# Ranks for the mixers' small matmuls, products grouped by tile size, and activation tiles moved to one byte remainder

## The chip, the cores and the metric

The kernel runs on one core of one Trainium2 chip. The metric is device time in microseconds (us) of one launch; the runs shown are medians of repeated launches. Engines are named as the profile names them: PE (TensorE matmul), PEld (TensorE weight load), DVE (VectorE), ACT (ScalarE), POOL (GpSimd), SP (the queue that issues most DMAs).

## The reference

One sequence of 256 positions and width 1024 passes through two model blocks, all in float32.

- The first block has two layers. A layer is a SwiGLU feed-forward (inner width 2816) added with weight 0.5, then a mixer, then a second such feed-forward. The mixer projects the normalized input to three groups of heads, runs them side by side (16 heads of a Mamba-2 state-space form in chunks of 128, called ssd; 4 mLSTM heads of 128; 8 RWKV-7 heads of 64) and projects their outputs back.
- The second block is one layer: a modulation from a vector `c`, eight attention heads of 64 beside a gated convolution, an output projection, and a feed-forward with a 3-tap convolution.

The part of ssd that the change rewrites is, per chunk of 128 positions and per head,

```
y_diag = einsum(cb * decay, x_dt)        # within a chunk
y_off  = einsum(C, state_before) * exp(a_cum)   # from the state before the chunk
y      = y_diag + y_off + X * d_skip
```

## The kernel before, in words

Activations are kept transposed: 128 features on the partitions, 256 positions along the row. A weight matrix is cut into 128x128 blocks, 3,808 in all, streamed in chunks of seven (`raw`, 448 KB) by SP. `chunk` (L126) splits a chunk into a rounded high part `whi` (ACT, L134) and the rest `wlo` (DVE, L135). `mm` (L151) then issues three matmuls for one block, all of 128x128 weights against 256 columns: high by high (L153), high by low (L154), low by high (L155). The activations they multiply lie in tiles that hold a high and a low part: `pair0` and `pair1` (a normalized input), `hp` (the hidden layer of a feed-forward, 22 blocks of 256 columns, one tile in each of the five feed-forwards), and ring tiles `w` in a mixer. They are called weight matmuls below, 11,424 in all. Every other matmul is small, in plain float32, and part of some chain of dependent steps.

The mixer (`mixers`, L385) weaves five chains into the projections: `rwkv` twice (L518, four heads each), `gates` (L795), `ssd` (L980), `mlstm` (L849). Each chain is a generator that yields an estimated cost; `weave` (L487) resumes the chain whose estimated time is least if that is not later than the projections' own estimated time, else it writes the next projection. So the program text alternates. The order in which instructions stand on an engine is then set by the Tile framework's scheduler: among instructions that its own model of the program holds ready, the one with the lowest rank goes first, and the rank is the position in the written order. `tc.high_priority(n)` lowers the rank by n. Before, a chain's step is moved up by `BOOST`, one position (L500). Each engine then runs its instructions strictly in that order.

The steps named below: in `rwkv`, L691 multiplies the pieces of a 64x64 triangular inverse (its input comes from a solve in 15 steps on DVE and a reordering on ACT), L704 and L705 finish a level; L633 and L642 are small sums and transposes; then a recurrence over four chunks runs L726/L729 (products into `x1`), a copy `R` on ACT (L732), L736, a copy on ACT (L737), L742 and L754, and the new state on DVE (L747, L750). In `ssd`, for each of four groups of four heads, L1064 and L1066 are the products within the first and the second chunk and L1068 the product with the state.

A matmul uses only part of the array if it has fewer than 128 rows to sum over or fewer than 128 outputs. The profile prints this part as rows*columns: weight matmuls 128*128, L1064 and L1066 128*64 (64 outputs), L1068, L691, L704, L705, L729 and L736 64*64, L601 64*128. This is called the tile size below.

`gap` (L258) allocates an unused tile of n bytes per partition in a pool and clears it on POOL. It shifts the start of all tiles that are allocated behind it. As built, `whi` and `wlo` start 160 bytes past a multiple of 256; the starts of the activation tiles are listed with the change. The calls that the change resizes are at L324, L397, L1164, L1271, L1314 and L1316.

Of the kernel before, what the change touches and what calls it, by code (L numbers as in the profile page):

```python
# [16 lines left out]
T = 256  # L17
# [20 lines left out]
GD_AHEAD = 1  # L38
BOOST = (1, 1, 1, 1, 1)
DENSE = 0.34  # L40
GAPS = {"xg": 448, "xn": 192, "mix": 288, "ffn": (384, 128, 448, 192, 448), "attn": 256}
W_OUT = ((("rwkv0", "rwkv1"), (12, 13, 14, 15)), (("ssd",), (0, 1, 2, 3, 4, 5, 6, 7)), (("mlstm",), (8, 9, 10, 11)))

IN_PAIRS = "k0 r0 v0 r2 k2 v2 xb8 xb0 dtg xb2 xb4 xb6 z0 z2 z4 xm0 z6 xm2 o0 o2".split()
# [33 lines left out]
def _program(tc, a, order, dbg=None):  # L78
    nc = tc.nc
    es = ExitStack()  # L80
    dbg = dbg or (lambda name, ap: None)
    V, S, G, PE = nc.vector, nc.scalar, nc.gpsimd, nc.tensor

    def pool(name, bufs=1, **kw):
        return es.enter_context(tc.tile_pool(name=name, bufs=bufs, **kw))
# [19 lines left out]
    p = ps.tile([128, 512], F32, name="st")  # L105
# [3 lines left out]
    def P(name, j=0, n=1):  # L109
        c = PCOL[name] + j  # L110
        return par[:, c:c + n]
# [96 lines left out]
    def mps(shape=(128, 512), tag="m"):  # L208
        return ps.tile(list(shape), F32, name=tag, bufs=4 if tag == "m" else 1)
# [48 lines left out]
    def gap(pool, n):  # L258
        if n:
            turn.append(0)  # L260
            G.memset(pool.tile([128, n // 4], F32, name=f"gap{len(turn)}"), 0.0)
# [3 lines left out]
    def pair(dtype=F32R):  # L265
        pairs.append(0)
        return act.tile([128, 2, DT, T], dtype, name=f"pair{len(pairs) % 2}")
# [4 lines left out]
    def new_acc():  # L272
        return act.tile([128, 2, T], F32, name="acc", bufs=2)
# [21 lines left out]
    def cut(t, js):  # L295
        return t[:, js[0]:js[-1] + 1]
# [24 lines left out]
    def ffn(l, which, acc, xg, next_gain):  # L321
        with tc.tile_pool(name=f"ffn{which}{l}", bufs=1) as fp:
            gu, dn = f"ffn{which}_w_gate_up", f"ffn{which}_w_down"
            gap(fp, GAPS["ffn"][2 * l + which - 1])  # L324
            hp = fp.tile([128, 2, FT, T], F32R, name="hp")
# [56 lines left out]
    def bc(ap, shape):  # L382
        return ap.to_broadcast(shape)

    def mixers(l, acc, xg):  # L385
# [10 lines left out]

        gap(mp, GAPS["mix"])  # L397
        nka = mp.tile([128, 4], F32, name="nka")
# [79 lines left out]
        for i, (need, ks) in enumerate(W_OUT):  # L478
            last = i == len(W_OUT) - 1
            for js in OUTS if last else ((0, 1), (2, 3), (4, 5), (6, 7)):  # L480
                work.append((None, need, DENSE * len(ks) * len(js), lambda js=js, ks=ks, last=last: w_out(js, ks, last)))
        weave(work, [rwkv(l, 0, mp, ring, b), rwkv(l, 1, mp, ring, b), gates(l, mp, ring, b),
                     ssd(l, mp, ring, b), mlstm(l, mp, ring, weight, b)])
        mx.close()
        return nxt

    def weave(work, gens):  # L487
        done, now = {}, 0.0
        chains = [[0.0, g, None, i] for i, g in enumerate(gens)]
        work = list(work)  # L490
        while work or chains:
            free = [c for c in chains if c[2] is None or c[2] in done]
            c = min(free, key=lambda c: max(c[0], done.get(c[2], 0.0))) if free else None
            if c:
                c[0] = max(c[0], done.get(c[2], 0.0))
            ready = work and all(n in done for n in work[0][1])
            if c and (not ready or c[0] <= now):
                c[2] = None
                try:
                    with tc.high_priority(BOOST[c[3]]):  # L500
                        r = next(c[1])
                except StopIteration as e:
                    chains.remove(c)
                    done[e.value] = c[0]
                    continue
                if isinstance(r, str):
                    c[2] = r
                else:
                    c[0] += r * CHAIN
            else:  # L510
                name, need, cost, fn = work.pop(0)
                now = max([now] + [done[n] for n in need])
                fn()
                now += cost
                if name:
                    done[name] = now
# [463 lines left out]
    def ssd(l, mp, ring, b):  # L980
# [4 lines left out]
        for c in range(2):  # L985
            for g in range(2):
                gs = slice(g * 64, g * 64 + 64)
# [6 lines left out]
        p = mps()  # L994
# [8 lines left out]
        ea = [ring(128, 4, 128) for _ in range(2)]  # L1003
# [7 lines left out]
        xdt = {}  # L1011
        pst = mps()
        for g in range(2):
            yield f"xb{4 * g + 2}"
            hs = slice(g * 8, g * 8 + 8)
            for c in range(2):
                p = mps()
# [11 lines left out]
        st = ring(128, 8, 64)  # L1029
# [8 lines left out]
        def load(q):  # L1038
            if q < 4:
                gds[q] = [ring(128, 4, 128) for _ in range(2)]  # L1040
                for c, t in enumerate(gds[q]):
                    nc.sync.dma_start(t, da[q * 4:q * 4 + 4, c * 128:c * 128 + 128].unsqueeze(0)
                                      .to_broadcast([128, 4, 128]))
# [3 lines left out]
        for q in range(4):  # L1047
            g = q // 2
            gs = slice(g * 64, g * 64 + 64)
            load(q + GD_AHEAD)  # L1050
            gd = gds[q]
            for c, t in enumerate(gd):
                for h in range(4):
                    S.activation(t[:, h], t[:, h], AF.Relu, scale=-1.0, bias=nat[:, c, q * 4 + h:q * 4 + h + 1])
                S.activation(t, t, AF.Exp, scale=-1.0)
                V.tensor_mul(t, t, bc(cbm[:, c, g:g + 1], [128, 4, 128]))
                yield 2.0
            js = (2 * q, 2 * q + 1)
            p = mps()
            for u, i in enumerate(js):  # L1060
                for j in range(2):
                    h = 2 * i + j
                    o = p[j * 64:j * 64 + 64, u * T:u * T + T]
                    PE.matmul(o[:, 0:128], xdt[0, g][:, h % 8], gd[0][:, h % 4], start=(u == 0), stop=True,  # L1064
                              skip_group_check=True)
                    PE.matmul(o[:, 128:256], xdt[1, g][:, h % 8], gd[1][:, h % 4], start=False, stop=False,  # L1066
                              skip_group_check=True)
                    PE.matmul(o[:, 128:256], st[gs, h % 8], ea[h % 8 // 4][gs, h % 4], start=False, stop=True,  # L1068
                              skip_group_check=True)
            for u, i in enumerate(js):  # L1070
                V.scalar_tensor_tensor(xs[:, i], xs[:, i], P(f"ssd_d{l}", i), p[:, u * T:u * T + T],
                                       op0=OP.mult, op1=OP.add)
            yield f"z{2 * q}"
            V.tensor_mul(cut(xs, js), cut(xs, js), cut(b["sz"], js))
            if q % 2 == 0:
                S.activation(accs[g], cut(xs, js), AF.Square)
            else:
                sq = ring(128, 2, T)
                S.activation(sq, cut(xs, js), AF.Square)
                V.tensor_add(accs[g], accs[g], sq)  # L1080
            yield 2.0
# [57 lines left out]
    def modulate(rb, gain, shift):  # L1139
        xn = pair()  # L1140
        for j in range(DT):
            n = tmp()[:, 0]
            V.scalar_tensor_tensor(n, x[:, j], gain[:, j:j + 1], rb, op0=OP.mult, op1=OP.mult)
            S.activation(xn[:, 0, j], n, AF.Identity, bias=shift[:, j:j + 1])
            V.scalar_tensor_tensor(xn[:, 1, j], n, shift[:, j:j + 1], xn[:, 0, j].bitcast(F32),
                                   op0=OP.add, op1=OP.subtract)
        return xn
# [12 lines left out]
    def second(accs, xg):  # L1160
        rb, rb2 = stat_rstd(accs, D, EPS, chain=True)
        with tc.tile_pool(name="attn", bufs=1) as mp:
            xn = modulate(rb2, a1[:, 0], mod[:, 0:8])
            gap(mp, GAPS["attn"])  # L1164
            mixed = [mp.tile([128, 2, 4, T], F32R, name=f"m{i}") for i in range(2)]
# [102 lines left out]
        with tc.tile_pool(name="ffn_2", bufs=1) as fp:  # L1268
            rb, = stat_rstd([acc], D, EPS)
            xn = modulate(rb, a1[:, 1], mod[:, 24:32])  # L1270
            gap(fp, GAPS["ffn"][4])  # L1271
            hp = fp.tile([128, 2, FT, T], F32R, name="hp")
# [40 lines left out]
    acc = new_acc()  # L1313
    gap(act, GAPS["xg"])  # L1314
    xg = pair()
    gap(act, GAPS["xn"])  # L1316
    for j in range(0, DT, 2):
# [8 lines left out]
    later = None  # L1326
    for l in range(LAYERS):
        acc, xg = ffn(l, 1, acc, xg, f"mix_norm{l}")
        dbg(f"xa{l}", x)
        acc, xg = mixers(l, acc, xg)  # L1330
        dbg(f"xb{l}", x)
        if l == LAYERS - 1:
            later = pool("later")
            ab = later.tile([128, 8, 384], F32, name="ab")
        acc, xg = ffn(l, 2, acc, xg, f"ffn1_norm{l + 1}" if l + 1 < LAYERS else None)
        dbg(f"xc{l}", x)
# [161 lines left out]
```

## Time and profile before

| | us |
|---|---|
| median of 3 runs | 1627.86 (1627.2 to 1629.0) |
| the profiled execution, its own time | 1627.1 |
| its span from first to last instruction | 1625.3 |
| PE busy | 1584.9 (98%), 13,660 records |
| PEld busy | 1516.4 (93%) |
| DVE busy | 1161.4 (71%) |
| ACT busy | 1000.1 (62%) |
| POOL busy | 47.5 (3%) |

The profiled execution's own time is 1.8 us above its span, and 0.8 us below the median of the runs. Matmuls overlap in the array, so a busy PE is no PE at its peak: the distance from one matmul's start to the next one's tells more than its duration. A small float32 matmul leaves two records, a transpose one. The program goes through: feed-forward of layer 0 to 196 us, mixer to 474, feed-forward to 658, feed-forward of layer 1 to 845, mixer to 1119, feed-forward to 1306, attention to 1437, last feed-forward to the end.

### The profile page before, as it was taken

Reading aid. Unit: us, or ns where it says so; the run is one execution under the profiler, and the core shown is the slowest. Engines: PE = TensorE matmul, PEld = TensorE weight load, DVE = VectorE, ACT = ScalarE, POOL = GpSimd, SP = SyncE. Lnnn points to the kernel's source line nnn. Section 1 sums busy time; section 2 is a strip of 40 time slices with the busy share of each in tenths; the row PEclk is TensorE's granted clock in tenths of the full one; section 3 lists DMA queues with packets and bytes.
Section 4 is the critical chain, followed back from the end, with each engine's and each line's share of the span. In section 5 each row is a group of like instructions: output and inputs, shape, how many; then the busy total and the mean of one; then the engine's idle time right before and its main releaser. Section 6 shows DMA issues by size and latency. Waiting matters only on the chain.

```text
span 1625.3 us, 33775 instructions
## 1 busy us (share of the span) xinstructions
PE 1584.9 (98%) x13660; PEld 1516.4 (93%) x13660; DVE 1161.4 (71%) x1965; ACT 1000.1 (62%) x1692; POOL 47.5 (3%) x68
## 2 busy tenths in 40 slices
PE   8999999999999999999999899999999999999998
PEld 7999988878999999999998887799999998999997
DVE  7865679856787755787568975688785676798853
ACT  6554576887655454545458788765554566587753
POOL 0000001000000000000000100000000000000000
PEclk9999989999999999999999999999999999999999
DMA  7866633333357766597563333436886653556662
GB/s 252 306 195 190 204 118 123 101 112 116 115 181 244 242 187 194 185 329 260 183 194 125 115 106 117 127 117 216 288 306 185 185 166 113 159 162 190 187 189 72
DMA packets 106717, 290.81 MB, mean 179 GB/s; under 512 B 15640, under 2 KB 28096, under 8 KB 106432
## 3 DMA queue, kind: packets, MB, share of 16 engines
q1 hardware_dynamic: 106272, 288.12, 55.9%
q8 instruction: 107, 1.75, 0.4%
q10 hardware_dynamic: 288, 0.52, 0.1%
q14 instruction: 50, 0.41, 0.1%
HBM read 287.51 MB, written 1.09 MB: 178 GB/s over the span
## 4 chain that ended last, share of the span: by engine, by line
PE 77%; issue 13%; DVE 5%; ACT 2%; DMA 1%; POOL 1%; SPq 0%; DVEq 0%; POOLq 0%; ACTq 0%
PE d L155 21%; PE d L153 21%; PE d L154 21%; DVE wlo L135 1%; DMA ada<-ada 1%; PE m L691 1%; PE m L754 1%; PE m L1064 1%; POOL stm L212 1%; PE m L1068 1%; PE m L736 1%; PE st L221 1%; PE m L705 1%; ACT whi L134 1%; PE m L1066 1%
## 5 line engine op out<-in xcount | busy, mean ns | idle before, releaser
L135 DVE TENSOR_TENSOR wlo<-raw,whi 128x896 fp32r<-128x896 f32 x544 | 590.4, 1089 | 245.1 <-ACT whi L134 242.3
L153 PE MATMUL d<-pair,whi 128*128 128x256 f32 x2672 | 753.2, 282 | 4.8 <-ACT whi L134 2.1
L155 PE MATMUL d<-pair,wlo 128*128 128x256 f32 x2672 | 753.8, 282 | 1.8 <-DVE wlo L135 1.8
L154 PE MATMUL d<-pair,whi 128*128 128x256 f32 x2672 | 752.9, 282 | 0.1
L134 ACT CAST whi<-raw 128x896 fp32r<-128x896 f32 x544 | 511.5, 943 | 348.3 <-PE d L154 254.0
L153 PEld LDWEIGHTS d<-pair,whi 128*128 128x128 f32 x2672 | 508.8, 190 | 14.8 <-issue 5.9
L155 PEld LDWEIGHTS d<-pair,wlo 128*128 128x128 f32 x2672 | 508.1, 190 | 7.2 <-DVE wlo L135 2.9
L154 PEld LDWEIGHTS d<-pair,whi 128*128 128x128 f32 x2672 | 508.5, 190 | 3.0 <-issue 1.4
L154 PE MATMUL d<-hp,whi 128*128 128x256 f32 x880 | 246.6, 280 | 0.0
L155 PE MATMUL d<-hp,wlo 128*128 128x256 f32 x880 | 246.1, 280 | 0.0
L153 PE MATMUL d<-hp,whi 128*128 128x256 f32 x880 | 246.1, 280 | 0.0
L155 PEld LDWEIGHTS d<-hp,wlo 128*128 128x128 f32 x880 | 166.2, 189 | 0.0
L154 PEld LDWEIGHTS d<-hp,whi 128*128 128x128 f32 x880 | 166.1, 189 | 0.0
L153 PEld LDWEIGHTS d<-hp,whi 128*128 128x128 f32 x880 | 166.1, 189 | 0.0
L205 ACT CAST hp<-h 128x256 fp32r<-128x256 f32 x88 | 35.4, 406 | 90.9 <-DVE h L345 90.8
L1124 DVE SCALAR_TENSOR_TENSOR adasum<-ada,sc,adasum 128x1024 f32<-128x1024 f32 x42 | 53.8, 1281 | 14.4 <-DMA ada<-ada 14.4
L206 DVE TENSOR_TENSOR hp<-h,hp 128x256 fp32r<-128x256 f32 x88 | 36.7, 421 | 15.3 <-ACT hp L205 14.5
L1157 DVE SCALAR_TENSOR_TENSOR up<-raw,par,up 128x255 f32<-128x255 f32 (+1 forms) x88 | 37.2, 480 | 10.6 <-ACT raw L1153 10.3
L344 ACT ACTIVATE s<-d 128x256 f32<-128x256 f32 x80 | 30.2, 378 | 23.3 <-PE d L155 22.2
L345 DVE TENSOR_TENSOR h<-s,d 128x256 f32<-128x256 f32 x88 | 36.0, 415 | 3.8 <-ACT s L344 3.8
L155 PE MATMUL d<-w,wlo 128*128 128x256 f32 x128 | 37.1, 290 | 0.0
L154 PE MATMUL d<-w,whi 128*128 128x256 f32 x128 | 37.1, 290 | 0.0
(403 smaller groups left out, 1829.0 us busy)
## 6 DMA issues: line engine op xcount, KB each, us to landing
raw<-ws SPq DMA_DIRECT2D x544, 448.0 KB, 3.7
ada<-ada SPq DMA_DIRECT2D x48, 512.0 KB, 5.9
w<-da SPq DMA_DIRECT2D x16, 256.0 KB, 5.1
w<-small SPq DMA_DIRECT2D x10, 256.0 KB, 3.9
ab<-abias SPq DMA_DIRECT2D x1, 1536.0 KB, 7.1
x<-xT SPq DMA_DIRECT2D x4, 256.0 KB, 4.9
w<-da SPq DMA_DIRECT2D x8, 128.0 KB, 3.6
w<-dw SPq DMA_DIRECT2D x4, 256.0 KB, 5.5
```

Of the source, the lines that this page charges most:

```text
L134: S.copy(hi, raw)
L135: V.tensor_sub(lo, raw, hi.bitcast(F32))
L153: PE.matmul(p, h, xh, start=start, stop=False, skip_group_check=True)
L154: PE.matmul(p, h, xl, start=False, stop=False, skip_group_check=True)
L155: PE.matmul(p, lo, xh, start=False, stop=stop, skip_group_check=True)
L205: S.copy(hi, src)
L206: V.tensor_sub(lo, src, hi.bitcast(F32))
L212: G.tensor_tensor(dst, m, mhalf.to_broadcast([128, n]), op=OP.pow)
L344: S.activation(s, p[:, 0], AF.Silu)
L345: V.tensor_mul(h, s, p[:, 1])
L1124: V.scalar_tensor_tensor(acc, w, sc[:, k:k + 1], acc, op0=OP.mult, op1=OP.add)
L1157: V.scalar_tensor_tensor(dst[:, i, d:], raw[:, i, :T - d], P(w, 3 * j + k), dst[:, i, d:], op0=OP.mult, op1=OP.add)
```

## The change

Three edits.

1. Ranks. `PE` becomes an object whose `matmul` and `transpose` pass through `first`. While `weave` resumes a chain, `PE.chain` is set, and each small matmul of the chain gets a rank far ahead of all others (100,000 less its running number, so that the written order is kept among them). So a chain's matmul that the scheduler's model holds ready goes ahead of every weight matmul, and ahead of matmuls of other chains that were written later.
2. The ssd products. For each group of four heads, all eight products within the chunks are issued first, and the four products with the state behind them. It was one head after the other.
3. Gaps. Sizes change, one is added (`later`), two become nothing.

```diff
-GAPS = {"xg": 448, "xn": 192, "mix": 288, "ffn": (384, 128, 448, 192, 448), "attn": 256}
+AHEAD_PE = 100000
+GAPS = {"xg": 192, "xn": 192, "mix": 32, "ffn": (128, 128, 128, 0, 0), "attn": 0, "later": 256}
...
-    V, S, G, PE = nc.vector, nc.scalar, nc.gpsimd, nc.tensor
+    V, S, G = nc.vector, nc.scalar, nc.gpsimd
+
+    class Ordered:
+
+        chain = False
+        n = 0
+
+        def first(self, op, *args, **kw):
+            if not self.chain:
+                return op(*args, **kw)
+            self.n += 1
+            with tc.high_priority(AHEAD_PE - self.n):
+                return op(*args, **kw)
+
+        def matmul(self, *args, **kw):
+            return self.first(nc.tensor.matmul, *args, **kw)
+
+        def transpose(self, *args, **kw):
+            return self.first(nc.tensor.transpose, *args, **kw)
+
+    PE = Ordered()
...
                 try:
+                    PE.chain = True
                     with tc.high_priority(BOOST[c[3]]):
                         r = next(c[1])
...
+                finally:
+                    PE.chain = False
...
-            for u, i in enumerate(js):
-                for j in range(2):
-                    h = 2 * i + j
-                    o = p[j * 64:j * 64 + 64, u * T:u * T + T]
-                    PE.matmul(o[:, 0:128], xdt[0, g][:, h % 8], gd[0][:, h % 4], start=(u == 0), stop=True,
-                              skip_group_check=True)
-                    PE.matmul(o[:, 128:256], xdt[1, g][:, h % 8], gd[1][:, h % 4], start=False, stop=False,
-                              skip_group_check=True)
-                    PE.matmul(o[:, 128:256], st[gs, h % 8], ea[h % 8 // 4][gs, h % 4], start=False, stop=True,
-                              skip_group_check=True)
+            cells = [(2 * i + j, p[j * 64:j * 64 + 64, u * T:u * T + T], u) for j in range(2) for u, i in enumerate(js)]
+            for h, o, u in cells:
+                for c in range(2):
+                    PE.matmul(o[:, c * 128:c * 128 + 128], xdt[c, g][:, h % 8], gd[c][:, h % 4], start=(u == c == 0),
+                              stop=(c == 0), skip_group_check=True)
+            for h, o, u in cells:
+                PE.matmul(o[:, 128:256], st[gs, h % 8], ea[h % 8 // 4][gs, h % 4], start=False, stop=True,
+                          skip_group_check=True)
...
             later = pool("later")
+            gap(later, GAPS["later"])
```

No matmul is added or removed: 11,424 weight matmuls and 1,246 small ones stand in both programs. Since every call now passes through `first`, all matmuls of the new program carry the lines 92 (no chain) and 95 (in a chain).

**Order on PE.** Neighbours on PE that differ in tile size: 376 places before, 232 now (280 with the ranks alone). All of the difference lies in the mixers, 169 and 97 in each: 16 and 12 ahead of the first L691, 48 and 32 from there to the second rwkv chain's first L691, 105 and 53 behind that. The first L691 stands behind 2,104 weight matmuls before and behind 2,119 now; the second chain's behind 2,296 and 2,332. Three places follow, all in the mixer of layer 0.

On PE, the first group of ssd products, before (`w_4321` and the like are ring tiles, `S` and `am` are rwkv's):

```order
L1068 MATMUL m<-w_3975,w_4297 64x128
L726 MATMUL m<-S,w_3291 128x128
L1064 MATMUL m<-w_4321,w_3989 64x128
L729 MATMUL m<-w_3682,am 64x64
L1066 MATMUL m<-w_4322,w_4010 64x128
L729 MATMUL m<-w_3682,am 64x64
L1068 MATMUL m<-w_3975,w_4297 64x128
L729 MATMUL m<-w_3682,am 64x64
L1064 MATMUL m<-w_4321,w_3989 64x128
L729 MATMUL m<-w_3682,am 64x64
L1066 MATMUL m<-w_4322,w_4010 64x128
L1068 MATMUL m<-w_3975,w_4297 64x128
```

and now:

```order
L95 MATMUL m<-R,w_3949 64x64 x4
L95 MATMUL m<-w_4322,w_4010 64x128
L95 MATMUL m<-w_4321,w_3989 64x128
L95 MATMUL m<-w_4322,w_4010 64x128
L95 MATMUL m<-w_4321,w_3989 64x128
L95 MATMUL m<-w_4322,w_4010 64x128
L95 MATMUL m<-w_4321,w_3989 64x128
L95 MATMUL m<-w_4322,w_4010 64x128
L95 MATMUL m<-w_3975,w_4297 64x128 x4
L95 MATMUL m<-w_3682,w_3648 128x128 x2
L95 MATMUL m<-w_3682,am 64x64 x4
```

The products of one tile size stand together, and rwkv's four products stand ahead of them or behind, not between.

On PE, the second level of the first rwkv chain, whose L691 stands beside sums of the second chain (L633, input `rki`), before:

```order
L691 MATMUL m<-w_3296,am 64x64 x2
L633 MATMUL m<-rki,w_3075 128x2
L691 MATMUL m<-w_3296,am 64x64
L633 MATMUL m<-rki,w_3075 128x2
L691 MATMUL m<-w_3296,am 64x64
L633 MATMUL m<-rki,w_3075 128x2
L691 MATMUL m<-w_3296,am 64x64
L633 MATMUL m<-rki,w_3075 128x2
L691 MATMUL m<-w_3296,am 64x64 x11
```

and now:

```order
L95 MATMUL m<-w_3296,am 64x64 x16
L95 MATMUL m<-rki,w_3075 128x2 x4
L95 MATMUL m<-cst,w_3288 128x128
L95 MATMUL m<-cst,w_3289 128x128
```

Eight changes between 64*64 and 128*128 have become one.

On ACT, the two copies of the first recurrence step (`R`, and the next, which writes `w_3155`), before:

```order
L732 COPY R<-m 64x256
L656 COPY w_3682<-m 64x256
L657 COPY w_3682<-m 64x256
L380 ACT_TABLE_LOAD
L380 ACTIVATE pair_3252<-pair_3252 128x512
L656 COPY w_3683<-m 64x256
L657 COPY w_3683<-m 64x256
L821 COPY w_3698<-w_3695 16x256
L374 COPY w_3782<-d 128x512
L826 COPY w_3565<-w_3531 4x256
L737 ACTIVATE w_3155<-m 64x256
```

and now:

```order
L756 COPY R<-m 64x256
L761 ACTIVATE w_3155<-m 64x256
L401 ACT_TABLE_LOAD
L401 ACTIVATE pair_3252<-pair_3252 128x512
L680 COPY w_3682<-m 64x256
```

The second copy has moved up past nine instructions, to the place right behind the first. On PE the four products of L736 stood 15 weight matmuls behind L729's and 27 ahead of L742; now it is 4 and 4. In each mixer eight steps of the recurrences now stand at most five weight matmuls behind the step that they need; before there were two.

**Starts of the activation tiles**, in bytes past a multiple of 256, as built:

| tile (weight matmuls that read it) | before | now |
|---|---|---|
| `pair0`, `pair1`, the mixers' ring tiles, the attention's `m0`, `m1` (8,592 in all) | 96 | 96 |
| `hp` of the first two feed-forwards (2 x 528) | 96 | 96 |
| `hp`, layer 1, first feed-forward, from 782 us (528) | 160 | 96 |
| `hp`, layer 1, second feed-forward, from 1243 us (528) | 32 | 96 |
| `hp`, last feed-forward, from 1551 us (528) | 32 | 96 |
| `xgh`, `xgl`, 258 columns, in the attention and last feed-forward (192) | other | the same |

The two high or low halves of all these tiles keep that remainder. The order of DMAs on SP differs in eight places by one position; POOL clears fewer bytes of gaps.

## Rows read from the trace of the kernel before

**Rows 1.** The page, parts 1 and 2: busy time of each engine, and the granted clock.

```profile
PE 1584.9 (98%) x13660; PEld 1516.4 (93%) x13660; DVE 1161.4 (71%) x1965; ACT 1000.1 (62%) x1692; POOL 47.5 (3%) x68
...
PEclk9999989999999999999999999999999999999999
```

**Rows 2.** Busy time by stretch (us, busy and count per engine, clock, DMA): both mixers.

```profile
196.00:474.00 278.00, 267.77 (x2345) 241.81 (x2344) 207.84 (x427) 204.45 (x370) 18.37 (x23) 0.96 0.41 125
846.00:1119.00 273.00, 262.95 (x2340) 238.13 (x2340) 207.32 (x427) 204.06 (x369) 18.32 (x23) 0.98 0.42 127
```

**Rows 3.** What PE waited for from 196 to 474 us: sum, times, longest.

```profile
PE m L691 <- issue: 3.8, 2, 2.4
PE m L556 <- ACT w L551: 2.5, 2, 1.4
```

**Rows 4.** Timeline of PE, ssd's second group: start, duration, rows*columns of the array.

```profile
380.49 0.38 PE L1066 MATMUL m<-w,w 128*64 128x128 f32 x2
380.80 0.43 PE L1068 MATMUL m<-w,w 64*64 64x128 f32 x2
381.16 0.43 PE L1064 MATMUL m<-w,w 128*64 128x128 f32 x2
381.43 0.38 PE L1066 MATMUL m<-w,w 128*64 128x128 f32 x2
```

**Rows 5.** Timeline of PE in the attention: three products of one tile size.

```profile
1339.57 0.38 PE L1215 MATMUL m<-sT,vn 128*64 128x128 f32 x2
1339.79 0.38 PE L1216 MATMUL m<-sT,vn 128*64 128x128 f32 x2
1340.10 0.48 PE L1197 MATMUL m<-qk 64*128 64x128 f32 x2
```

**Rows 6.** Timeline of PE: L691 in one run, then L691 between L633.

```profile
285.65 1.15 PE L691 MATMUL m<-w,am 64*64 64x64 f32 x32 [2.39 <-issue]
286.73 0.45 PE L154 MATMUL d<-pair,whi 128*128 128x256 f32 x1
...
294.22 0.33 PE L691 MATMUL m<-w,am 64*64 64x64 f32 x4
...
296.50 1.02 PE L691 MATMUL m<-w,am 64*64 64x64 f32 x22
```

**Rows 7.** Timeline of PE: 64*64 products of two chains at once.

```profile
302.38 0.22 PE L729 MATMUL m<-w,am 64*64 64x64 f32 x1
302.38 0.22 PE L705 MATMUL m<-w,w 64*64 64x64 f32 x1
```

**Rows 8.** Timeline of PE: 128*128 products with one weight matmul between two.

```profile
435.97 0.38 PE L944 MATMUL m<-vn,w 128*128 128x129 f32 x2
...
436.31 0.38 PE L944 MATMUL m<-vn,w 128*128 128x129 f32 x2
```

**Rows 9.** Busy time by stretch: `hp` four times, `pair0` twice (first count: weight matmuls).

```profile
140.00:190.00 50.00, 50.00 (x443) 50.00 (x443) 28.91 (x34) 24.53 (x32) 0.00 (x0) 1.00 0.64 193
790.00:840.00 50.00, 50.00 (x419) 50.00 (x418) 28.25 (x34) 23.53 (x32) 0.00 (x0) 1.00 0.59 184
1250.00:1300.00 50.00, 50.00 (x423) 50.00 (x423) 28.94 (x35) 25.71 (x38) 0.00 (x0) 1.00 0.61 184
1555.00:1600.00 45.00, 45.00 (x378) 44.55 (x377) 23.09 (x27) 19.39 (x25) 0.00 (x0) 1.00 0.53 164
690.00:770.00 80.00, 80.00 (x709) 79.43 (x708) 63.19 (x80) 40.33 (x63) 0.00 (x0) 1.00 0.85 296
1460.00:1540.00 80.00, 80.00 (x681) 80.00 (x681) 68.94 (x125) 61.55 (x109) 0.00 (x0) 1.00 0.60 186
```

**Rows 10.** Busy time in one of seven stretches at half clock, behind the first L691.

```profile
286.90:290.30 3.40, 3.40 (x17) 3.40 (x18) 3.40 (x6) 3.37 (x8) 0.00 (x0) 0.50 0.21 42
```

**Rows 11.** Timeline of ACT: the two copies of the first recurrence step.

```profile
302.92 0.37 ACT L732 COPY R<-m 64x256 f32<-64x256 f32 x1
...
308.24 0.38 ACT L737 ACTIVATE w<-m 64x256 f32<-64x256 f32 x1
```

## The prediction

> **What bounds the kernel now.** I read the busy times first. PE is busy for 98% of the span and its clock is granted almost everywhere; no other engine passes 71% [rows 1]. So the end is set by what PE does and by what it waits for. The stretches say where PE is not at its best: the two mixers take 278 and 273 us with PE idle for about 10 us each, and at a mean clock of 0.96 and 0.98 [rows 2]. [...] The waits [rows 3] are few: L691 3.8 us in two waits, L556 2.5 us. That is little against 278 us. The rest of a mixer is PE's own work, so the spacing of its matmuls is what to read next.
>
> A weight matmul has 256 columns. Their spacing in stretches without a gap is in the busy times by stretch [rows 9]; a count takes in about two that only overlap the ends, so I take two off. In the first `hp` stretch 50 us hold 441, 113.4 ns each. The other three `hp` stretches hold 417, 421 and (in 45 us) 376: 119.9, 118.8 and 119.7 ns. The load of DVE, ACT and DMA is the same in the first two of these rows (28.9 and 28.3 us, 24.5 and 23.5 us, 0.64 and 0.59), the clock too. What differs is the start of `hp`: 96 bytes past a multiple of 256 in the first, 160, 32 and 32 in the others. With `pair0`, at 96 both times, one stretch runs at 113.2 ns (707 in 80 us), another at 117.8 (679). So remainder 96 allows the short spacing and doesn't secure it.
>
> **The tile sizes.** In the attention a small product is followed by one of the same size after 0.22 us, by one of another size after 0.31 [rows 5]: 0.09 for the switch. In ssd [rows 4] L1066 ahead of another size takes 0.31, L1064 behind one 0.27, so the first product after a switch pays 0.05 more. A change costs 0.14 us. A second place [rows 6]: five L691 and four L633 with eight changes take 2.28 us (294.22 to 296.50). Sixteen L691 in one run take 1.08, so five take 0.34; four L633 at 0.22 take 0.88; 1.06 is left, 0.13 per change. A switch between weight and small matmuls of one tile size costs nothing: a product and a weight matmul together take 0.34 us [rows 8], which is 0.22 and 0.11.
>
> Ranks and regrouping take out 144 changes, 72 per mixer. The lower end is the switch alone, 0.09: 13.0 us. The upper end: 64*64 products in different quarters of the array start together [rows 7], while L1068, alone between other sizes, takes 0.36 [rows 4]; if such a product becomes free in a group, two changes give back 0.36, 0.18 each: 25.9 us. I take 0.15, near the 0.14 of ssd [rows 4], since those are the very products: **144 x 0.15 = 21.6 us less**.
>
> Does it reach the end? Of the 72 in a mixer, 52 lie behind the second chain's first L691, where no long wait is left. Sixteen lie between the two first L691 and save 2.4 us ahead of the second, which waited 1.4 us (3.8 less 2.4) [rows 3, 6]. But 36 more weight matmuls now stand ahead of it, 36 x 0.113 = 4.1 us of work that fills 2.4 + 1.4. The first L691 waited 2.4 us; 15 more weight matmuls (1.7 us) stand before it against 0.6 us saved, so some 1.3 us of wait stays. I count the whole 21.6.
>
> **Waits that are added.** A chain's matmul now stands as early as the scheduler's model holds it ready, and behind it on PE stand all weight matmuls. The eight close steps per mixer have at most five weight matmuls, 0.57 us, for a copy on ACT of 0.37 us [rows 11] and the hand-overs. Before, the second copy began 5.3 us after the first began (302.92 to 308.24); in the new order it stands right behind, so ACT's queue is no longer in the way. A hand-over isn't in the rows; I bound the wait of one such step by 0 and 0.6 us (a step may just miss one cast) and take 0.3: 16 x 0.3 = 4.8 us for both mixers. The first two L691 wait 1.1 and 1.4 us less, 5.0 us in both mixers. These cancel. A stretch of 3.4 us at half clock, as behind the first L691, holds 16 or 17 matmuls, 0.21 us each [rows 10], and so costs 3.4 x (1 - 0.113/0.21) = 1.6 us; I allow for one more of them: **1.6 us more**. Bounds: 5 us less (the shorter waits alone), 8 us more (every close step at 0.6, less nothing).
>
> **The starts.** Three `hp` tiles come to remainder 96. The one from 782 us follows a `pair0` stretch at 113.2 ns: 528 x (119.9 - 113.4) = 3.4 us. The one from 1243 us: 528 x (118.8 - 113.4) = 2.9. The last one follows the `pair0` stretch at 117.8 ns, so I let it run at that: 528 x (119.7 - 117.8) = 1.0. **7.3 us less**. Ends: all three at 117.8 give 2.6, all at 113.4 give 9.6; beyond that, a stage of 960 weight matmuls that stays at 96 may pass from one spacing to the other, 960 x 4.4 ns = 4.2 us either way.
>
> [...]
>
> The gaps cost nothing elsewhere: POOL is busy for 3% [rows 1] and clears less. SP's eight moved DMAs are raw chunks that go one place earlier or later, six chunks ahead of use. The changed order on ACT and DVE is covered by their idle time in the mixers, 278 - 204 and 278 - 208 us [rows 2]; without that cover a cast that is late by one copy (0.37) would stop PE.
>
> **Sum.** 1627.1 (the profiled execution's own time) - 21.6 - 7.3 + 1.6 = 1599.8; the median of the runs lies 0.8 above that execution, so **1600.6 us**.
>
> **The rivals.**
> 1. *Early ranks make PE wait in order, slower.* A chain's matmul stands in front, its copy on ACT is behind a cast, and the weight matmuls that used to run meanwhile are queued behind it. One such event, as the first L691 shows, costs 2.4 us and a half-clock stretch, 4.0 in all [rows 6, 10]. It decides from 28.9 / 4.0, seven events; five per mixer give 40 - 28.9 = 11 us more: 1639. For it: eight close steps per mixer. Against: L736 and L742, of which two were as close before, are missing among the waits [rows 3]. 5%.
> 2. *Starts don't matter*, and the `hp` stretches differ for another reason. Then 1627.9 - 21.6 + 1.6 = 1607.9. Against it the equal load [rows 9]; for it the two `pair0` rows. 8%.
> 3. *PE's saved time comes back as waits for the chains.* The recurrences have a length of their own on ACT and DVE; if only half of the 104 late changes shows, 7.8 us: 1627.9 - 7.8 - 7.3 + 1.6 = 1614.4. For it: L691 waits already. Against: the weight matmuls that moved ahead. 17%.
> 4. *All terms at their good ends:* 1627.9 - 25.9 - 9.6 - 5 = 1587.4. For it the overlap [rows 7], as it is more frequent in groups. 12%.
> 5. *Nothing comes of it:* ranks and starts are changed in the built order, so only equal gains and losses would do. 3%.
>
> **How the numbers follow.** The forecast has 55%; its own range is 1592 to 1610. The range to 8 in 10 takes in rival 3 and nearly rival 4: 1588 to 1616. A measurement of this kernel can tell about 0.2%, 3.3 us, from no change. Faster: 55 + 8 + 17 + 12 = 92%; same 3%; slower 5%.
>
> **What would show it.** Weight matmuls per 50 us in the two `hp` stages of layer 1 should be 441 (rival 2: 417 to 421). The mixers should be 265 and 260 us, some 12 us shorter each, with the idle time of PE near 10 us; in rival 3 they keep more of their length and the waits for ACT and DVE grow, in rival 1 those at L736's and L742's places are long and the mean clock falls below 0.96. The ssd group should show products 0.22 us apart and one switch. I am wrong if the mixers aren't shorter by at least 4 us each.

## The result, and the profile after

The changed kernel takes 1608.26 us (median of 4 runs, 1607.38 to 1615.12) against 1628.02 us before in the same measurement: ratio 0.9888 (0.9860 to 0.9915), 19.8 us less, where 27.3 us less was forecast. The total lies in the predicted range. As the sections below show, it does so in part by luck, because two wrong terms partly cancel: the regrouped ssd products gave nearly twice what was put down, the ranks as a whole gave nothing. That nothing is itself a sum: the ranks of the ssd chain gave 12.9 us, those of the other chains cost 10.8 (experiments 3 and 4).

The profiled execution is the slowest of the four: 1615.12 us, span 1613.3. The lines of the page that answer to [rows 1]:

```profile
PE 1561.7 (97%) x13660; PEld 1509.1 (94%) x13660; DVE 1161.1 (72%) x1965; ACT 990.7 (61%) x1684; POOL 44.6 (3%) x66
...
PEclk9999999899999999999999989999999999999999
```

PE is busy for 23.2 us less than before, yet the span is only 12.0 us shorter: part of the saved work came back as idle time. Busy time by stretch (us, busy and count per engine, clock, DMA share, GB/s): first the two mixers, cut at the same weight matmuls as [rows 2], then the `hp` stretches of layer 1 and of the end, as in [rows 9].

```profile
195.90:466.60 270.70, 254.80 (x2345) 237.22 (x2344) 207.87 (x427) 199.22 (x365) 17.14 (x23) 0.97 0.42 128
838.30:1107.50 269.20, 254.20 (x2341) 236.69 (x2342) 207.68 (x427) 198.75 (x365) 17.01 (x22) 0.97 0.43 129
775.00:825.00 50.00, 50.00 (x444) 50.00 (x443) 27.90 (x32) 24.24 (x32) 0.00 (x0) 1.00 0.63 191
1230.00:1280.00 50.00, 50.00 (x444) 50.00 (x443) 29.27 (x35) 26.08 (x39) 0.00 (x0) 1.00 0.64 194
1550.00:1595.00 45.00, 44.96 (x382) 44.13 (x381) 22.21 (x26) 20.96 (x27) 0.00 (x0) 1.00 0.46 138
```

The mixers are 7.3 and 3.8 us shorter, 11.1 together. PE's busy time in them fell by 13.0 and 8.8 us, 21.7 together, but its idle time rose from 10.2 and 10.1 us to 15.9 and 15.0. The `hp` stretches of layer 1 now hold 444 weight matmuls in 50 us instead of 419 and 423. From their first weight matmul to their last, the three `hp` stages are 3.5, 2.8 and 1.2 us shorter.

What PE waited for in the first mixer, as in [rows 3]:

```profile
PE m L95 <- issue: 5.5, 3, 2.2
PE m L95 <- ACT w L575: 2.2, 2, 1.2
PE m L95 <- DVE w L989: 1.9, 1, 1.9
PE d L92 <- DVE wlo L156: 1.2, 1, 1.2
```

By source line, the first row is three waits of the rwkv chains' inverse levels: two at L715 (L691 before), of 1.85 and 1.50 us, and a new one of 2.2 us at L729 (L705 before). The third row is new too: mlstm's L994 waits for a result on DVE. The fourth is a weight matmul that waits for its own `wlo` cast.

The page names no releaser for L729 ("issue"), but the timelines of ACT and PE show one. L729 reads the tile that ACT's two copies at L723 write. They stand behind a table load and an activation of the `gates` chain (L830); the second ends at 295.74 us, and L729 starts 0.10 us later:

```profile
292.89 1.28 ACT L830 ACT_TABLE_LOAD   x1
295.38 0.36 ACT L723 COPY w<-m 32x256 f32<-32x256 f32 x1
295.84 1.03 PE L95 MATMUL m<-w,w 64*64 64x64 f32 x28 [2.17 <-issue]
```

So the rank moved the product forward on PE, while the copies that it needs still stand behind the `gates` chain on ACT, as before the change (L699 behind L806).

The ssd products, timeline of PE. First the ranks alone (a kernel of the experiments), then the changed kernel: the same group of 12 products with the same two matmuls behind it, 28 records, and the weight matmul that follows.

```profile
376.57 4.47 PE L95 MATMUL m<-w,w 128*64 128x128 f32 x28
380.80 0.49 PE L92 MATMUL d<-pair,whi 128*128 128x256 f32 x2
```

```profile
375.25 2.81 PE L95 MATMUL m<-w,w 128*64 128x128 f32 x28
377.82 0.48 PE L92 MATMUL d<-pair,whi 128*128 128x256 f32 x2
```

From start to next weight matmul: 4.23 us in the order head by head, 2.57 in the order by kind. The regrouping alone is worth 1.66 us per group. From the first product of a group to what follows its last, all eight groups of the two traces differ by that much. With four groups per mixer that makes 6.6 us per mixer, 13.3 in all.

Elsewhere the profiled execution lost time that the change did not cause by an instruction of its own. The second feed-forward of layer 0 is 3.1 us longer, since its `pair` tile, at remainder 96 (its start lies 96 bytes past a multiple of 256) before and now, ran at the long spacing (117.6 ns, against 113.4 in layer 1) here. The attention is 3.8 us longer, most of it in two stretches of 3.4 us at half clock (an estimated 1.6 us each, by the price from [rows 10]). The first two rows are the same stage in layer 0 and layer 1 of this one execution; the third is a half-clock stretch in the attention.

```profile
480.00:580.00 100.00, 98.48 (x838) 98.28 (x837) 68.07 (x92) 51.08 (x82) 0.00 (x0) 1.00 0.71 227
1120.00:1220.00 100.00, 99.82 (x880) 98.98 (x879) 78.64 (x106) 53.92 (x86) 0.00 (x0) 1.00 0.80 274
1369.30:1372.60 3.30, 3.30 (x18) 3.30 (x17) 1.67 (x4) 0.77 (x2) 0.00 (x0) 0.51 0.42 139
```

### The profile page after: what moved, and what is told of

It is laid out like the page before. It is cut to its first block, busy times and chain, and to the rows that moved or that the text cites. A ratio compares the mean times of both kernels' runs of the same rounds, so it can differ in the third digit from the quotient of the medians.

```text
span 1613.3 us, 33769 instructions
## 1 busy us (share of the span) xinstructions
PE 1561.7 (97%) x13660; PEld 1509.1 (94%) x13660; DVE 1161.1 (72%) x1965; ACT 990.7 (61%) x1684; POOL 44.6 (3%) x66
## 4 chain that ended last, share of the span: by engine, by line
PE 71%; issue 16%; DVE 6%; ACT 5%; POOL 1%; DMA 0%; DVEq 0%; POOLq 0%; SPq 0%; ACTq 0%
PE d L92 60%; PE m L95 8%; PE m L92 3%; DVE wlo L156 1%; ACT whi L155 1%; PE st L92 1%; POOL stm L233 1%; ACT w L699 1%; DVE am L628 0%; DVE pair L227 0%; DVE tmp L338 0%; DVE w L399 0%; DVE pair L399 0%; ACT w L426 0%; DMA x<-xT 0%
## 5 line engine op out<-in xcount | busy, mean ns | idle before, releaser
L92 PE MATMUL d<-pair,whi 128*128 128x256 f32 x5344 | 960.3, 282 | 4.8 <-ACT whi L155 2.2
L92 PEld LDWEIGHTS d<-pair,whi 128*128 128x128 f32 x5344 | 824.3, 190 | 17.0 <-issue 6.3
L92 PE MATMUL d<-hp,whi 128*128 128x256 f32 x1760 | 302.7, 277 | 0.0
L92 PEld LDWEIGHTS d<-hp,whi 128*128 128x128 f32 x1760 | 265.9, 188 | 0.0
L95 PE MATMUL m<-w,w 64*64 64x64 f32 (+5 forms) x848 | 66.9, 260 | 8.1 <-issue 4.3
L95 PEld LDWEIGHTS m<-w,w 64*64 64x64 f32 (+3 forms) x848 | 55.6, 155 | 15.3 <-issue 11.9
L95 PE MATMUL m<-cst,w 128*128 128x128 f32 (+1 forms) x166 | 29.6, 297 | 11.0 <-DVE w L989 4.1
L95 PE MATMUL m<-w,am 64*64 64x64 f32 (+1 forms) x512 | 33.7, 230 | 6.7 <-issue 6.7
L95 PEld LDWEIGHTS m<-w,am 64*64 64x64 f32 (+1 forms) x512 | 27.4, 140 | 13.4 <-issue 9.2
L92 PEld LDWEIGHTS d<-w,whi 128*128 128x128 f32 x256 | 39.1, 189 | 0.0
```

The source lines that it names most:

```text
L92: return op(*args, **kw)
L95: return op(*args, **kw)
```

## The experiments

Every time is a median, beside runs of the kernel before on the same chip (1626.7 to 1627.8 us in the four batches). Line numbers are those of the changed kernel.

**1. The gaps alone.**

```diff
-GAPS = {"xg": 448, "xn": 192, "mix": 288, "ffn": (384, 128, 448, 192, 448), "attn": 256}
+GAPS = {"xg": 192, "xn": 192, "mix": 32, "ffn": (128, 128, 128, 0, 0), "attn": 0, "later": 256}
...
             later = pool("later")
+            gap(later, GAPS["later"])
```

> The kernel before with the change's gaps alone; ranks and ssd order stay as before. The prediction's term for the starts: 7.3 us less, so 1628.0 - 7.3 = 1620.7 (bounds 2.6 to 9.6 less: 1625.4 to 1618.4), with the three hp stretches of layer 1 and of the end near 113.4, 113.4 and 117.8 ns per weight matmul. The traces of before and after, cut at the same weight matmuls, give 3.2, 2.6 and 1.2 us for these three stretches, 7.0 together: 1621.0. Rival 2 (starts don't matter): 1628.0, with the three stretches at 118.8 to 119.9 ns.

Measured: 1620.59 us (11 runs), ratio 0.9955 (0.9932 to 0.9979). Its three changed `hp` stretches, as in [rows 9]:

```profile
780.00:830.00 50.00, 50.00 (x444) 50.00 (x443) 27.65 (x32) 23.76 (x31) 0.00 (x0) 1.00 0.62 190
1235.00:1285.00 50.00, 50.00 (x446) 49.73 (x439) 27.83 (x34) 25.28 (x36) 0.00 (x0) 1.00 0.63 192
1550.00:1595.00 45.00, 44.96 (x394) 44.42 (x393) 24.39 (x30) 21.06 (x28) 0.00 (x0) 1.00 0.55 168
```

Starts matter, and by the predicted amount (6.6 us less, 7.3 forecast). The last stretch ran nearer the short spacing here (394 in 45 us, against 382 in the changed kernel's profile).

**2. The ranks alone** (the change without the new gaps and the new ssd order).

```diff
+    PE = Ordered()
...
+                    PE.chain = True
```

> The kernel before with the ranks alone: 96 tile-size changes fewer, gaps and ssd order as before. Theory A, the prediction's steps: 96 x 0.15 = 14.4 us less, 1.6 more for waits: 1628.0 - 12.8 = 1615.2. Theory B, formed from the traces of before and after: a mixer is only 7.3 and 4.0 us shorter; four whole groups of 12 ssd products take 2.10 us each in place of 3.76 in the old order, 6.6 us per mixer from the order of the ssd products alone; so ranks by themselves give 11.3 - 13.2 = -1.9, that is nothing: the time they save goes into new waits of PE (2.45, 2.19 and 1.43 us in the first mixer). 1624 to 1632, middle 1629.9.

Measured: 1629.82 us (12 runs), ratio 1.0019 (0.9998 to 1.0041). The ranks alone, on the old order of the ssd products, don't make the kernel faster. Both mixers, cut as above:

```profile
195.40:470.30 274.90, 259.49 (x2346) 237.34 (x2345) 207.60 (x427) 199.68 (x365) 17.17 (x23) 0.97 0.42 126
843.80:1119.40 275.60, 257.77 (x2341) 236.23 (x2341) 207.37 (x427) 199.40 (x365) 17.10 (x23) 0.98 0.41 125
```

PE's busy time fell by 8.3 and 5.2 us, 13.5 in all, close to the 14.4 of the prediction. Idle time rose to 15.4 and 17.8 us, 13.0 in all. The granted clock of the two profiles is nearly the same in the mixers (0.97 and 0.98 against 0.96 and 0.98 [rows 2]), so it does not explain this.

**3. The change without the ranks.**

```diff
-                    PE.chain = True
```

> The changed kernel without the ranks: gaps and the new ssd order stay; 114 tile-size changes more than with ranks. Theory A: 1608.3 + 114 x 0.15 - 1.6 = 1623.8. Theory B: ranks by themselves are worth nothing, but they keep the ssd groups whole; without them 23 of 48 products per mixer stand in pieces of 6, 9 and 8, so about half of the 6.6 us per mixer is left, 3.2 us: 1628.0 - 7.0 - 6.4 = 1614.6.

Measured: 1610.4 us (6 runs), ratio 0.9879 (0.9852 to 0.9906). That is the time of the whole change. Theory A (1623.8) is refuted. B is closer, but it expected 13.4 us less and 16.8 were measured; these 3.4 us are not explained. The change has this time with 114 tile-size changes fewer.

**4. Ranks for ssd alone.**

```diff
-                    PE.chain = True
+                    PE.chain = c[3] == 3
```

> The changed kernel with ranks for the ssd chain alone; the matmuls of rwkv, gates and mlstm are not ranked. 48 tile-size changes more than with all ranks. Theory A: 1608.3 + 48 x 0.15 = 1615.5, up to 1.6 less for waits that go. Theory B: the ssd groups stay whole (13.2 us), the gaps stay (7.0), and the new waits of rwkv and mlstm (L715, L729 and L994 in the changed kernel) go: 1628.0 - 13.2 - 7.0 = 1607.8, the same as with all ranks or up to 4 us faster.

Measured: 1597.49 us (6 runs), ratio 0.9819 (0.9786 to 0.9851). The mixers:

```profile
195.20:460.60 265.40, 252.10 (x2346) 233.44 (x2345) 207.79 (x427) 201.28 (x368) 17.38 (x23) 0.99 0.42 131
830.50:1095.00 264.50, 253.37 (x2342) 234.50 (x2342) 207.44 (x427) 201.29 (x367) 17.32 (x23) 0.98 0.43 131
```

With 48 tile-size changes more than the changed kernel it is 10.8 us faster, below both theories (B ended at 1603.8). The ranks of the other chains cost time. Those of ssd gain it: against experiment 3, with no ranks, this kernel is 12.9 us faster.

**5 and 6. Whose ranks cost it.** First all but rwkv's, then ssd's and rwkv's.

```diff
-                    PE.chain = True
+                    PE.chain = c[3] >= 2
...
+                    PE.chain = c[3] in (0, 1, 3)
```

> The changed kernel with ranks for ssd, gates and mlstm; rwkv not ranked. Which ranks cost the 10.8 us that lie between all ranks (1608.3) and ranks for ssd alone (1597.5)? Theory R, rwkv's: in the changed kernel PE waits 2.45 us at L729 and stays at half clock for 10.2 us behind it in each mixer, and neither is there with ranks for ssd alone: then this kernel takes 1597.5 to 1600. Theory M, mlstm's (the wait of 2.19 us at L994): 1605 to 1608. Half each: 1603. The prediction's steps (10 changes more than ssd alone, 0.15 each): 1599.0.

> The changed kernel with ranks for ssd and the two rwkv chains; gates and mlstm not ranked. Theory R: 1605 to 1609, with the wait at L729 and the long half-clock stretch back. Theory M: 1597 to 1600. Half each: 1603. The prediction's steps (44 changes fewer than with ranks for ssd alone, 0.15 each): 1597.5 - 6.6 = 1590.9.

Measured: 1602.12 us without rwkv's ranks (5 runs), 1608.39 with ssd's and rwkv's (5 runs). Without rwkv's ranks 6.2 of the 10.8 us come back, with them the whole loss is there, so most of it belongs to rwkv. The first value lies 2 us above theory R, nearest to "half each"; as its bounds overlap those of experiment 4, a part for mlstm and gates is not shown. The second refutes the prediction's steps (1590.9). Theory R's sign came only in part in its profile: PE waits 2.44 us at L729 in both mixers, but the stretch of 10.2 us at half clock follows in the second alone.

**7. ssd products in alternating halves of the array** (on top of ranks for ssd alone).

```diff
-            cells = [(2 * i + j, ..., u) for j in range(2) for u, i in enumerate(js)]
-            for h, o, u in cells:
-                for c in range(2):
+            cells = [(2 * i + j, ..., u) for u, i in enumerate(js) for j in range(2)]
+            for c in range(2):
+                for h, o, u in cells:
```

> Ranks for ssd alone, and inside a group of 12 ssd products the eight 128x64 ones alternate between the two column halves of the array (the same number of tile-size changes). In the ssd-only run such a group takes 1.9 to 2.1 us, and where its order passes from one half to the other the products start 0.11 us apart instead of 0.22. Theory O (a group is short because products in different halves overlap): eight products at about 0.12 in place of 1.52 us together, some 0.5 us less per group, four groups per mixer: 4 us less, 1593.5. Theory K (only the number of changes counts, the engine pairs the halves by itself): 1597.5, groups as long as before.

Measured: 1598.38 us (4 runs), ratio 0.9818 (0.9794 to 0.9843). Timeline of PE: the first row of each fence holds the eight 128*64 products of the second group and one state product, the second row starts right behind the start of the latter. Ranks for ssd alone, then with alternating halves:

```profile
374.79 1.84 PE L95 MATMUL m<-w,w 128*64 128x128 f32 x18
376.32 0.33 PE L92 MATMUL m<-R,w 64*64 64x64 f32 x2
```

```profile
374.97 1.35 PE L95 MATMUL m<-w,w 128*64 128x128 f32 x18
376.02 0.33 PE L92 MATMUL m<-R,w 64*64 64x64 f32 x2
```

Theory O is right on the row: 1.05 us instead of 1.53 from the first of the eight to that row. The time does not show it; its bounds are wider than the 4 us in question. In the profile the two mixers together are 1.0 us shorter (264.9 and 264.0). The halves are those of `j`: outputs on partitions 0 to 63 and on 64 to 127. Products that alternate between them start closer together in these two rows; the rows don't show why.

**8. All streamed tiles at remainder 0** (ranks for ssd alone, first gap 160 bytes larger).

```diff
-GAPS = {"xg": 192,
+GAPS = {"xg": 352,
```

> Ranks for ssd alone, and all streamed tiles moved up by 160 bytes, so that 11232 weight matmuls start at remainder 0 in place of 96. Known so far: at 96 either 113.3 or 117.8 ns per weight matmul, at 32 and 160 118.7 to 120. If 0 is like 32 and 160: 11232 x some 5 ns = 56 us more, about 1653. If it is always at the short spacing: the stretches now at 117.8 fall to 113.3, some 15 us less, about 1582. If 0 is like 96: 1597.5 within 8 us. Starts don't matter: 1597.5 too, but then the hp stretches of the runs so far stay unexplained.

One run: 1647.92 us. Two stretches without a gap, then both mixers:

```profile
70.00:120.00 50.00, 50.00 (x419) 50.00 (x418) 30.14 (x39) 23.82 (x39) 0.00 (x0) 1.00 0.62 193
600.00:650.00 50.00, 50.00 (x419) 50.00 (x418) 26.03 (x30) 22.10 (x28) 0.00 (x0) 1.00 0.59 183
```

```profile
204.70:471.90 267.20, 257.74 (x2345) 239.41 (x2344) 207.93 (x427) 201.48 (x368) 17.39 (x23) 0.99 0.42 130
859.20:1127.00 267.80, 257.48 (x2342) 238.96 (x2342) 207.80 (x427) 201.26 (x367) 17.29 (x23) 0.99 0.42 129
```

419 per 50 us, 119.9 ns each: remainder 0 is like 160 (119.9 [rows 9]), not like 96 (113.2 to 117.8). The mixers tell a second thing. A mixer has about 1,370 weight matmuls; by the two kernels' times they ran at an estimated 115.4 ns on average in experiment 4 (119.9 less 50.4 us / 11,232), so 4.5 ns more for each would make it 6 us longer, but it is 1.8 and 3.3 us longer than in experiment 4, and PE's idle time fell from 13.3 and 11.1 us to 9.5 and 10.3. So in a mixer part of a change in PE's own work can be taken up by its waits for the chains, here in the direction of more work, in experiment 2 in that of less.

**9 and 10. Which step of rwkv.** All chains ranked, but first without the two inverse levels, then without the close steps (the recurrence's products).

```diff
             pz = mps()
+            PE.chain = False
             for g in range(8):
...
+            PE.chain = False
             x1 = mps()
```

(For 9 the line stands ahead of the loops at L715 and L728, for 10 ahead of each group of products in the loop over `c`.)

> The changed kernel, all chains ranked but for rwkv's two inverse levels (the matmuls at L715, L728 and L729), which stand as before. Over the executions so far the mean granted clock was 0.993 before (31), 0.9855 with all ranks (4), 0.987 with the ranks alone (12), 0.993 with ranks for ssd alone (6), 0.991 without rwkv's (5), 0.989 with ssd's and rwkv's (5): 0.0075 of 1610 us is 24 us more at half clock, about 11 us of time. Which ranked step of rwkv brings it? Theory I, the inverse levels: in the changed kernel PE waits 2.1 us at L715 and 2.45 us at L729, and a half-clock stretch follows each; then this kernel has a clock of 0.991 or more and takes 1597 to 1601. Theory C, the close steps (c loop): clock 0.985 to 0.988, 1606 to 1610. Spread over all ranked steps: 1603.

> The changed kernel, all chains ranked but for the matmuls of rwkv's close steps (c loop), which stand as before. Theory I: clock 0.985 to 0.988, 1606 to 1610, with the long half-clock stretch behind the wait at L729 still there. Theory C: clock 0.991 or more, 1597 to 1601. Spread: 1603. The prediction's first rival named these close steps.

**11. The change again.**

> The changed kernel as it is, on the chip and beside the runs of the two others. If the low clock belongs to the change and not to four executions: 1606 to 1612, clock 0.984 to 0.988, and in the profile a half-clock stretch of some 10 us in at least one mixer behind the wait at L729. If it was an accident: clock 0.990 to 0.993 and 1598 to 1602.

| kernel | us (runs) | mean granted clock over its runs |
|---|---|---|
| before, beside all experiments | 1626.7 to 1627.8 (51) | 0.992 |
| ranks alone | 1629.82 (12) | 0.987 |
| the change, both measurements | 1608.26, 1607.92 (10) | 0.986 |
| close steps unranked | 1606.13 (6) | 0.986 |
| inverse levels unranked | 1597.62 (5) | 0.994 |
| ranks for ssd alone | 1597.49 (6) | 0.993 |

The ratios of 9, 10 and 11 are 0.982 (0.9796 to 0.9843), 0.9859 (0.9832 to 0.9886) and 0.988 (0.9852 to 0.9909). These three ran beside each other on one chip, where the kernel before had a mean clock of 0.990 (11 runs). Theory I holds: leaving the matmuls of rwkv's two inverse levels unranked brings back the clock and 10 us. Without the close steps' ranks the low clock stays, and the profile has a half-clock stretch of 13.7 us behind the wait at L729 in each mixer. The low clock belongs to the change: its second profile has a stretch of 10.2 us there in both mixers, as the first. The mixers with the inverse levels unranked:

```profile
198.20:461.10 262.90, 244.36 (x2345) 228.40 (x2344) 207.68 (x427) 201.51 (x367) 17.51 (x23) 1.00 0.43 132
833.80:1097.40 263.60, 245.54 (x2341) 229.72 (x2341) 207.83 (x427) 201.37 (x367) 17.15 (x23) 0.99 0.43 132
```

Its waits are no shorter: PE is idle for 18.5 and 18.1 us. What went is half clock: this execution has one stretch of 3.4 us in its mixers, the profiled one of the change several that add up to 34 us. It is the one with the highest clock of its five (0.997). The same place, around the end of the wait at L729, in the changed kernel and then with the inverse levels unranked:

```profile
294.00:298.00 4.00, 2.16 (x34) 1.71 (x34) 2.59 (x7) 2.80 (x7) 0.00 (x0) 0.92 0.00 0
298.00:302.00 4.00, 4.00 (x22) 3.21 (x22) 2.90 (x5) 0.94 (x3) 0.53 (x1) 0.50 0.00 0
```

```profile
296.00:300.00 4.00, 2.13 (x37) 1.85 (x38) 3.13 (x9) 3.43 (x9) 0.00 (x0) 1.00 0.00 0
300.00:304.00 4.00, 4.00 (x49) 3.74 (x46) 3.74 (x12) 3.90 (x8) 0.53 (x1) 1.00 0.17 24
```

In the first, 22 matmul records take the 4 us that hold 49, not all of the same kinds, in the second. Why the clock falls in the one and holds in the other, these rows don't say: PE's busy time just before is the same (2.16 and 2.13 us), its wait nearly so (2.17 and 1.86 us). In experiment 6 a wait of 2.44 us at this place was followed by half clock in one mixer and by full clock in the other. So that the ranks of the inverse levels lower the mean clock is shown (0.986 with them, 0.994 without); how they do it stays open.

**12. Also without mlstm's ranks.**

```diff
-                    PE.chain = True
+                    PE.chain = c[3] != 4
```

> Ranks for ssd, gates and rwkv, but neither for rwkv's two inverse levels nor for mlstm; the same 222 tile-size changes as with the inverse levels alone unranked (1597.6). With mlstm ranked PE waits some 2.0 us at L994's place in each mixer, before the change it didn't. Theory W (a wait of PE removed is time gained): 2 x 1.7 us less, 1594.2. Theory F (the time returns as another wait, for the mixers' chains are at their own length): 1597.6 within 2. The clock should stay at 0.991 or more in both.

Measured: 1595.1 us (5 runs), ratio 0.9799 (0.9778 to 0.982), clock 0.992. The wait at mlstm is gone, but the mixers are no shorter in its profile (262.5 and 264.0 us), which speaks for F. The median is 2.5 us lower, nearer to W, but its bounds overlap those of experiment 9. Left open. This is the lowest median of the study, 12.8 us below the change.

## Why the prediction was right, and where it wasn't

**The starts: right.** 7.3 us forecast, 6.6 measured alone (experiment 1), 7.5 by the three stages in the profile. Rival 2 is refuted by experiments 1 and 8: a weight matmul takes 113.3 to 117.8 ns at remainder 96 and 119.9 at 0. Why the start matters, no run shows. The assumption that the last `hp` keeps the spacing of the stage ahead held in the profile (382 in 45 us, 118.4 ns, behind a long one). In experiment 1 both were short, so the 1.0 us of this term depends on the execution.

**The tile sizes: too much, and both parts wrong.** With the starts taken off, the change gave some 12.8 us, where 21.6 less 1.6 for waits were forecast. The step "144 x 0.15 = 21.6" took one price for all changes. For the 48 changes of the ssd groups it forecast 7.2 us; they gave 13.3 where the ranks keep the groups whole, 0.28 per change. The step took a product of the same size to cost 0.22 us, as in the attention [rows 5], and so saw only the switch and its 0.05. But in the changed kernel's groups products of one kind stand closer: twelve take 2.10 us, 0.175 each. The upper end had this for the 64*64 products only [rows 7], 0.18 per change; the 128*64 ones stand closer too, where the two halves alternate (1.05 us instead of 1.53, experiment 7).

For the 96 changes by the ranks the price was about right as PE's work: busy time fell by 13.5 us with the ranks alone, 14.4 forecast. But "Does it reach the end? ... I count the whole 21.6" is the step that failed. It rested on no long wait being left behind the second L691. The chains made new ones: L729 for its copies on ACT, mlstm's L994, a `wlo` cast (2.2, 1.9 and 1.2 us in the changed kernel's first mixer). Idle time rose by 13.0 us. Nor did the weight matmuls that moved ahead of the first two L691 fill their waits: these should have been 2.5 us shorter per mixer, but fell only from 3.8 to 3.35 us. Experiment 9 shows it again: it has 58 tile-size changes fewer than experiment 4 and a higher clock, PE's busy time in the mixers is 15.6 us less, but its idle time 12.2 us more, and the median is the same. This is rival 3's mechanism, nearly to the full; it had 17% and only half of the late changes. Rival 3's sum also leaves out the 40 earlier changes, 6.0 us at the same price; with them it gives 1608.4, which is what was measured, though not for its reason: half clock is an estimated 6 to 9 us of the loss (next paragraph).

**The waits added: mis-sized.** "A stretch of 3.4 us at half clock ... I allow for one more of them: 1.6 us". The mean clock over all runs fell from 0.992 to 0.986: 0.006 x 1615 x 2 = 19 us more at half clock (0.50 in [rows 10]). By the term's own price (1 - 0.113/0.21 = 0.46) this is an estimated 9 us (6 by the runs on one chip, from 0.990). Measured, the inverse levels' ranks cost 10.3 us (experiments 9 and 11). The place was wrong as well: the term and rival 1 looked at the close steps, but those are innocent (experiment 10), and the inverse levels bring it (experiment 9). Rival 1's pair of a wait and a half-clock stretch exists then, at L729, once in each mixer of the changed kernel's two profiles, with 10.2 us at half clock behind it.

**The marks.** The `hp` count came as predicted (444, where 441 was named). The mixers should have been 12 us shorter each with idle time near 10; they are 7.3 and 3.8 with 15 to 16. So the second misses the threshold of 4 that the prediction set for being wrong. The ssd group shows its one switch, but products closer than the 0.22 us named.

**In numbers**, from 1628: gaps -7, regrouping -13, ranks between -0.3 and +6.7 (experiment 2) give -20.3 to -13.3; measured -19.8. Measured in another order, the same steps read: starts -6.6 (experiment 1), the new ssd order without ranks -10.2 (3), ssd's ranks -12.9 (4), the other chains' ranks +10.8. The edits are not independent: the ssd order needs ssd's ranks to keep its groups whole.

## What to carry to other kernels

Group small products by tile kind inside one step, and keep the group whole: here it gave 1.66 us per group, more than its six switches at the forecast's 0.15 (0.9 us), as twelve products take 2.10 us there, less than 12 x 0.22 = 2.64. Don't move a chain's matmuls to the earliest place wholesale: what they read may stay where it is on another engine, as at L729 (a wait of 2.2 us for copies on ACT). Instead rank one chain at a time, and judge by PE's idle time and by the granted clock over several runs, not by the count of switches. When a stage already waits for chains on other engines, part of what PE saves there can come back as idle time: here half with the whole change (21.7 us saved, 11.1 kept), nearly all with the ranks alone (13.5 us saved, 13.0 more idle).

## What the runs showed of the hardware

- The start of the streamed tile: remainder 96 gives 113.3 or 117.8 ns per 256-column weight matmul, remainder 0 gives 119.9 (one run, 1647.9 us against 1597.5, with the first gap 160 bytes larger and nothing else changed). Which of the two comes at 96 changes within one execution: 838 and 880 weight matmuls in 100 us of the same stage in two layers. Its cause is open.
- Clock: where it falls differs between executions. The changed kernel's first half-clock stretch in the first mixer is at 284 us in one profile, at 227 in the other, while the mean of its runs stays between 0.983 and 0.990. So one profile does not price such a term; ten runs do.
